# Fourier tables in seven steps between the first loads, the last gate and value by token halves, and a fixed TensorE order through the convolution's second half

## The chip, the core and the metric

The program runs on one core of one Trainium2 chip. The metric is the device time in microseconds (us) of one execution; the time before is 1710.61 us, the median of three runs (1710.35 to 1713.78). The core's engines run side by side, each through its own list of instructions in order, and wait for each other by semaphores: TensorE (PE) multiplies matrices, VectorE (DVE) and ScalarE (ACT) work elementwise, GpSimd (POOL) fills tables, and SyncE's queue (SP) issues the loads.

## The reference

Two layers over 256 latent and 256 context tokens of width 1024. Layer 0 mixes tokens by a Conformer convolution, layer 1 by a bidirectional mLSTM; both are followed by a squared-ReLU MLP. The change touches layer 0's convolution and what comes just before it. In short:

```python
sh1, sc1, g1, sh2, sc2, g2 = adaln(c, ada_w[0], ada_b[0])   # the context has its own six, from c_ctx
u = h * (1 + sc1) + sh1
a = u @ w_pw1 + b_pw1
a = a[..., :1024] * sigmoid(a[..., 1024:])     # value times gate
a = dwconv(a, w_dw)       # 31 taps per channel; latent tokens in rows of 64, context as one row of 256
a = silu(layer_norm(a + b_dw, ln_g, ln_b))
y = a @ w_pw2 + b_pw2
h = layer_norm(ALPHA * h + g1 * y, ln1_g[0], ln1_b[0])
...
```

## The kernel before, in words

All 512 tokens (context in columns 0 to 255, latent in 256 to 511) stand as the free axis; channels stand in 8 tiles of 128 partitions. Matrix products run in three terms: weights and data are each split into a rounded part (`wh`, made by ACT in line 154) and a rest (`wl`, made by DVE in line 155), and `mm3` (lines 177, 180, 181) adds `wh` by `u`, `wh` by `u`'s rest, and `wl` by `u`. Weights come in loads of 1 MB into `raw`, which has three buffers; `wh` and `wl` have four each.

The scheduler decides the order on each engine from the order of the program and its own estimates; the order holds from then on. A matmul may be nailed to its place in the program's order (`keep_in_program_order`, while `pin[0]` is true).

**The start.** Eight rounds `f`: `start0(f)` loads a block of the adaLN weights, a tile of `x` and a block of the first gate and value weights (`wr`), and multiplies the adaLN block with the conditioning columns (`ada_mm`, line 319); DVE copies the sums out of PSUM (line 605); `start1` folds them (line 327), adds the biases (lines 610, 611) and makes `u[f]` and its rest (lines 522, 523, 525); `start2` adds the round's 12 matmuls to four accumulators. PE's order in a round is: fold, the adaLN products of the next round, the 12 matmuls of the round before. Ahead of all this in the program stand the Fourier tables: five tables of 128 x 128 in one tile, `tab`, computed by DVE as sines by a polynomial in lines 556 to 573. GpSimd then makes three masked copies of the first table (`ge32`, `lt32`, `ge96`).

**The first half of the convolution.** A `gemm_steps` loop makes the other 12 gate and value tiles in six groups of two: the even ones are gates (sigmoid on ACT, line 639), the odd ones values (line 643 on DVE multiplies value by gate; PE transposes the tile, line 646; ACT copies it to `A`, line 647, tokens on partitions). Between them DVE runs the row products of adaLN (`ada0.step`, line 379). Once four channel tiles are there, `spectral(0, tt)` convolves 512 channels of each block of 128 tokens: a forward transform (lines 661 and 666, an fp32 matmul by `F0` or a masked copy), a product with the transformed taps on DVE (lines 676, 677), an inverse transform (line 687; two matmuls on different columns of the array, which may run at the same time where they follow each other), and bias and statistics (lines 694, 695).

**The second half.** After the last group `spectral(1, tt)` does the same for the other 512 channels; `token_norm` computes mean and scale of two token blocks on DVE (lines 499 to 505 and around them) and applies them on ACT (line 709); `silu` transposes each channel tile back (line 729), applies gain, bias and SiLU, and splits the result; the gemm with `pw2` takes it, context half first. `ada_sh.mm()` multiplies two further adaLN blocks in that stretch.

## Time and profile before

| | |
|---|---|
| median of three runs | 1710.61 us |
| the profiled execution's own time | 1710.9 us |
| its span, first to last instruction | 1709.2 us |
| DVE busy in the span | 1095.9 us (64%) |
| ACT busy in the span | 743.3 us (43%) |
| GpSimd busy in the span | 33.5 us (2%) |
| DMA, mean over the span | 176 GB/s |

The chain of work that ended last is PE for 90% of the span, DVE for 4%, ACT for 3% and DMA for 2%. PE's row on the page counts modelled ends of pipelined matmuls, so it cannot tell a dense stretch from one at half the clock; windows and the timeline can. In the timeline a row gives start, duration, engine, line, operation, tiles written and read, form and count, and in brackets how long the engine idled before it and who ended that. An fp32 matmul shows as two records. In a windows row each engine's busy time and count stand in the order PE, PE's weight loads, DVE, ACT, POOL, followed by PE's granted clock, the DMA share and GB/s.

### The profile page before, as it was taken

To read this page: it belongs to the slowest core of one execution; us is meant where nothing else is said; L and a number is where in the kernel's file an instruction comes from. 1 tells how busy PE (TensorE), PEld (TensorE's weight loads), DVE (VectorE), ACT (ScalarE), POOL (GpSimd) and SP (SyncE) were. 2 spreads that over 40 slices of the span, in tenths; PEclk is the share of its full clock that TensorE was granted. 3 is DMA by queue.
4 is the path that set the end of the run, shared out by engine and by line. 5 is a ranking of instruction groups with operands and counts; after the bars stand their busy time and mean duration, and the time that the engine had idled before them with its cause. 6 is when DMAs were issued, how large, how long until landed. Compare 5 with 4: busy or idle time off the path is not lost.

```text
span 1709.2 us, 22611 instructions
## 1 busy us (share of the span) xinstructions
PE 1666.7 (98%) x8805; PEld 1365.7 (80%) x8805; DVE 1095.9 (64%) x1971; ACT 743.3 (43%) x1196; POOL 33.5 (2%) x84
## 2 busy tenths in 40 slices
PE   5999999999999999999999999999999999999998
PEld 3755788888888998876678889888867778888886
DVE  6895797975666686773132553453387786678765
ACT  2412565132324364643232543342276674555652
POOL 1000000000000000000000000000011110000000
PEclk9999999999999999999999999999999999999999
DMA  8634214555554236557663542253355545646651
GB/s 316 248 123 179 92 51 175 219 211 207 197 197 172 75 119 196 179 197 267 234 222 123 194 154 93 101 195 124 123 185 190 205 173 204 243 182 222 234 186 48
DMA packets 60666, 301.57 MB, mean 176 GB/s; under 512 B 6066, under 2 KB 20946, under 8 KB 27152
## 3 DMA queue, kind: packets, MB, share of 16 engines
q1 hardware_dynamic: 42832, 285.44, 46.0%
q10 hardware_dynamic: 17728, 14.70, 2.6%
q8 instruction: 69, 1.13, 0.3%
q14 instruction: 37, 0.30, 0.1%
HBM read 284.37 MB, written 15.75 MB: 176 GB/s over the span
## 4 chain that ended last, share of the span: by engine, by line
PE 90%; DVE 4%; ACT 3%; DMA 2%; issue 1%; POOL 0%; SPq 0%; DVEq 0%; ACTq 0%; POOLq 0%
PE mm L177 17%; PE mm L180 17%; PE mm L181 16%; PE mm L192 4%; PE mm L187 3%; PE mm L185 3%; PE mm L1544 3%; PE mm L186 3%; PE mm L196 2%; PE cv L185 2%; PE cv L187 2%; PE cv L186 2%; PE mm L1545 2%; PE cv L687 1%; DVE wl L155 1%; PE fl L797 1%
## 5 line engine op out<-in xcount | busy, mean ns | idle before, releaser
L155 DVE TENSOR_TENSOR wl<-raw,wh 128x1024 fp32r<-128x1024 f32 x346 | 422.0, 1224 | 303.9 <-ACT wh L154 301.3
L154 ACT CAST wh<-raw 128x1024 fp32r<-128x1024 f32 x346 | 360.9, 1052 | 508.8 <-PE mm L180 307.0
L180 PE MATMUL mm<-u,wh 128*128 128x512 f32 (+1 forms) x832 | 298.1, 360 | 0.0
L177 PE MATMUL mm<-u,wh 128*128 128x512 f32 (+1 forms) x704 | 248.1, 357 | 5.8 <-DVE E L967 3.3
L181 PE MATMUL mm<-u,wl 128*128 128x512 f32 (+1 forms) x704 | 248.1, 355 | 0.0
L180 PEld LDWEIGHTS mm<-u,wh 128*128 128x128 f32 x832 | 157.8, 190 | 24.0 <-issue 1.6
L177 PEld LDWEIGHTS mm<-u,wh 128*128 128x128 f32 x704 | 132.4, 190 | 31.8 <-issue 4.4
L181 PEld LDWEIGHTS mm<-u,wl 128*128 128x128 f32 x704 | 133.5, 190 | 19.8 <-issue 2.2
L177 PE MATMUL mm<-xm,wh 128*128 128x512 f32 x256 | 102.8, 402 | 0.0
L185 PE MATMUL mm<-wh,xl 128*128 128x512 f32 x256 | 101.2, 397 | 0.7 <-ACT wh L154 0.5
L186 PE MATMUL mm<-wh,xl 128*128 128x512 f32 x256 | 100.4, 392 | 0.6 <-DVE xl L155 0.6
L181 PE MATMUL mm<-xm,wl 128*128 128x512 f32 x256 | 100.3, 392 | 0.0
L187 PE MATMUL mm<-wl,xl 128*128 128x512 f32 x256 | 99.6, 394 | 0.3 <-DVE wl L155 0.2
L379 DVE CUSTOM_DVE_ANT_0 raw<-raw,cb,vecs 128x1024 f32<-128x1024 f32 x64 | 81.7, 1282 | 25.8 <-DMA raw<-adar_w 25.3
L177 PE MATMUL mm<-hid,wh 128*128 128x512 f32 (+1 forms) x256 | 93.2, 364 | 0.0
L180 PE MATMUL mm<-hid,wh 128*128 128x512 f32 (+1 forms) x256 | 92.8, 363 | 0.0
L181 PE MATMUL mm<-hid,wl 128*128 128x512 f32 (+1 forms) x256 | 92.8, 363 | 0.0
L1544 PE MATMUL mm<-x,wh 128*128 128x512 f32 x224 | 79.0, 397 | 0.0
L180 PE MATMUL mm<-qq,wh 128*128 128x272 f32 x256 | 73.9, 289 | 0.0
L177 PE MATMUL mm<-qq,wh 128*128 128x272 f32 x256 | 73.5, 289 | 0.0
L181 PE MATMUL mm<-qq,wl 128*128 128x272 f32 x256 | 73.5, 288 | 0.0
L192 PE MATMUL mm<-u,wh 128*128 128x512 f32 x192 | 68.4, 398 | 0.0
(490 smaller groups left out, 3277.8 us busy)
## 6 DMA issues: line engine op xcount, KB each, us to landing
raw<-w SPq DMA_DIRECT2D x64, 1024.0 KB, 4.8
raw<-adar_w SPq DMA_DIRECT2D x32, 1024.0 KB, 4.8
raw<-wo SPq DMA_DIRECT2D x32, 1024.0 KB, 4.8
raw<-ada_w SPq DMA_DIRECT2D x16, 1024.0 KB, 4.9
raw<-wv SPq DMA_DIRECT2D x16, 1024.0 KB, 5.3
raw<-wqT SPq DMA_DIRECT2D x16, 1024.0 KB, 5.8
raw<-wq SPq DMA_DIRECT2D x16, 1024.0 KB, 4.8
raw<-wk SPq DMA_DIRECT2D x16, 1024.0 KB, 4.8
```

The lines of the kernel that those rows point to most:

```text
L154: c = nc.scalar.copy(hi, src)
L155: nc.vector.tensor_tensor(lo, src, hi.bitcast(F32), op=ALU.subtract)
L177: a = nc.tensor.matmul(ps, wh, xh, start=start, stop=False)
L180: nc.tensor.matmul(ps, wh, xl, start=False, stop=False)
L181: nc.tensor.matmul(ps, wl, xh, start=False, stop=stop)
L185: nc.tensor.matmul(ps, xh, wh, start=start, stop=False)
L186: nc.tensor.matmul(ps, xl, wh, start=False, stop=False)
L187: nc.tensor.matmul(ps, xh, wl, start=False, stop=stop)
L192: nc.tensor.matmul(ps, wh, x, start=start, stop=stop)
L196: nc.tensor.matmul(ps[:, :C], wl, x[:, :C], start=False, stop=False)
L379: nc.vector.tensor_tensor_reduce(dump, w, cb[:, s, :], 1.0, vecs[:, o:o + 1], ALU.mult, ALU.add, accum_out=ada[self.l][:, m, s:s + 1])
L1544: a = lambda stop: nc.tensor.matmul(ps, wh, u2[kt], start=kt == 0, stop=stop)
```

## The change

Four edits in the function that builds the program.

1. The tables become a generator, `tables()`. Its body stands where the tables stood, but its steps run inside the start's rounds, one behind each `start2`; seven pieces in all, first the table arguments, then three pieces for `WC` and `WS`, then three for `F0`, `G1` and `G2` (before, `F0`, `G1` and `G2` came first). The masked copies move behind the start.
2. `spectral(0, tt)` is called one gemm tile later, behind tile 4 of the loop instead of inside the value tile 3, and the row products are dealt out as (1, 2, 1, 2, 2, 2, 2, 2, 1, 1) over ten tiles.
3. The sixth group of gate and value leaves the loop. Its two tiles are made in halves of 256 tokens, with matmuls of 256 columns, and sigmoid, product, transposes and copy work on a half each.
4. From there to the end of the adaLN products PE's order is nailed to the program's, which is written out by hand: the forward transforms of token blocks 0 and 1 between the halves of the last value tile, the inverse ones after it, and one `ada_sh.mm()` between the forward and inverse transforms of each of blocks 2 and 3. `silu(0)` follows, with its affine now on ACT for both halves, and `token_norm(2)` stands right behind it.

```diff
-    for t_ in (tab[:, 0:3 * L], tab[:, 3 * L:5 * L]):
...
+    def tables():
...
+        yield
+        for t_ in (tab[:, 3 * L:5 * L], tab[:, 0:3 * L]):
...
+            nc.vector.scalar_tensor_tensor(tz, t_, -1.0, t_, op0=ALU.mult, op1=ALU.max)
+            yield
...
+            nc.vector.scalar_tensor_tensor(tz, tz, SIN[4], sq_, op0=ALU.add, op1=ALU.mult)
+            yield
+            for k in (3, 2, 1):
+                nc.vector.scalar_tensor_tensor(tz, tz, SIN[k], sq_, op0=ALU.add, op1=ALU.mult)
+            nc.vector.scalar_tensor_tensor(t_, tz, SIN[0], t_, op0=ALU.add, op1=ALU.mult)
+            yield
+
+    tabs = tables()
...
         if f >= 2:
             start2(f - 2)
+            next(tabs, None)
     pin[0] = False
+    for _ in tabs:
+        pass
...
-        if f == 3:
-            for tt in range(4):
-                spectral(0, tt)
...
-            if s:
-                nc.scalar.activation(y, xn, AF.Identity, scale=V("cln_g", f), bias=V("cln_b", f))
-            else:
-                nc.vector.tensor_scalar(y, xn, V("cln_g", f), V("cln_b", f), op0=ALU.mult, op1=ALU.add)
+            nc.scalar.activation(y, xn, AF.Identity, scale=V("cln_g", f), bias=V("cln_b", f))
...
         pw1_epi(m + KO0, ps)
-        ada0.step(2 if m % 3 == 2 else 1)
+        if m == 4:
+            for tt in range(4):
+                for _ in spectral(0, tt):
+                    pass
+        ada0.step((1, 2, 1, 2, 2, 2, 2, 2, 1, 1)[m])
...
-    steps = gemm_steps(pw1, range(6), u, T, pw1_next)
+    steps = gemm_steps(pw1, range(5), u, T, pw1_next)
...
-    normed = None
-    for t0 in (0, 2):
-        for tt in (t0, t0 + 1):
-            spectral(1, tt, normed)
-        normed = token_norm(t0)
-        if t0 == 0:
-            for g in range(2):
-                pre_pw2(g)
-            for _ in silu(0):
-                pass
-    for i in range(2):
+    def pw1_part(m, s, kts=range(DT)):
+        sl = HALVES[s][1]
+        for kt in kts:
+            mm3(ps2[m][:, sl], *kcol(wl2[m], kt), *[t_[:, sl] for t_ in u[kt]], kt == 0, kt == DT - 1)
...
+    pin[0] = True
+    for m in range(2):
+        pw1_part(m, 0)
+        if m == 0:
+            part_epi(0, 0)
+    pw1_part(0, 1, range(4))
+    part_epi(1, 0)
+    pw1_part(0, 1, range(4, DT))
+    part_epi(0, 1)
+    pre_pw2(0)
+    sp = [spectral(1, tt, banks=("mm", "fl")) for tt in range(2)]
+    next(sp[0])
+    pw1_part(1, 1, range(4))
+    next(sp[1])
+    pw1_part(1, 1, range(4, DT))
+    for _ in sp[0]:
+        pass
+    part_epi(1, 1)
+    for _ in sp[1]:
+        pass
+    normed = token_norm(0)
+    pre_pw2(1)
+    for tt in (2, 3):
+        sp1 = spectral(1, tt, normed)
+        next(sp1)
         ada_sh.mm()
+        for _ in sp1:
+            pass
     ada_sh.end()
+    pin[0] = False
+    for _ in silu(0):
+        pass
+    token_norm(2)
```

DVE's list at the start of the program, before: `tab` and its helpers `F_143`, `F_157` are the tables, `fl_194` holds the sums of the first adaLN products, and `F_203` is their copy, which the first fold on PE reads.

```order
L568 TENSOR_SCALAR tab<-F_157 128x256
L572 SCALAR_TENSOR_TENSOR F_143<-F_143,F_144 128x384
L569 TENSOR_TENSOR F_158<-tab 128x256
L573 SCALAR_TENSOR_TENSOR tab<-F_143,tab 128x384
L570 TENSOR_SCALAR F_157<-F_158 128x256
L605 COPY F_203<-fl_194 128x256
L572 SCALAR_TENSOR_TENSOR F_157<-F_157,F_158 128x256
L610 TENSOR_SCALAR sh1p<-ln_205,vecs 128x2
```

The same place in the list now: the copy of the sums (line 600 of the changed kernel) stands behind the split of the first weight block and one multiplication for the tables.

```order
L551 TENSOR_SCALAR pc<-pc 128x1
L155 TENSOR_TENSOR wl_174<-wr_147,wh_173 128x512
L145 TENSOR_TENSOR foldg<-foldg,ident 128x16
L552 TENSOR_TENSOR pc<-pc 128x1
L557 TENSOR_SCALAR tab<-F_121,pc 128x128
L553 TENSOR_SCALAR pc<-pc 128x1
L600 COPY F_158<-fl_149 128x256
L558 TENSOR_SCALAR tab<-F_121,pc 128x128
L605 TENSOR_SCALAR sh1p<-ln_160,vecs 128x2
```

Of the 25 operations of the tables that stood ahead of the first copy one still does; the others stand behind it, spread over the rounds.

PE's list where the second half's normalized tokens come, before: `u_557` and `u_559` are the normalized blocks, which line 729 transposes, `cv_1358` and `cv_1377` the inverse transforms of blocks 2 and 3, `mm_1445` the first `pw2` tile.

```order
L327 MATMUL fl_1432<-fold,F_1430 128x4 x4
L729 MATMUL ln_1270<-ident,u_557 128x128
L729 MATMUL ln_1289<-ident,u_557 128x128
L666 MATMUL mm_1365<-A,tab 128x512
L729 MATMUL ln_1270<-ident,u_559 128x128
L729 MATMUL ln_1289<-ident,u_559 128x128
L687 MATMUL cv_1358<-F_1354,tab 64x512
L687 MATMUL cv_1358<-F_1350,tab 64x512
L687 MATMUL cv_1358<-F_1355,tab 64x512
L729 MATMUL ln_1270<-ident,u_557 128x128
L729 MATMUL ln_1270<-ident,u_559 128x128
L687 MATMUL cv_1358<-F_1351,tab 64x512
```

The same place now (the inverse transforms are line 701, the transposes line 743, the forward transforms line 680, `cv_1284` is token block 1 and `cv_1347` block 2):

```order
L701 MATMUL cv_1284<-F_1257,tab 64x512
L701 MATMUL cv_1284<-F_1253,tab 64x512
L680 MATMUL mm_1323<-A,tab 128x512
L680 MATMUL mm_1322<-A,tab 128x512
L319 MATMUL fl_1334<-raw_1335,cs 32x512 x4
L319 MATMUL fl_1334<-raw_1337,cs 32x512 x4
L743 MATMUL ln_1393<-ident,u_557 128x128
L743 MATMUL ln_1412<-ident,u_557 128x128
L743 MATMUL ln_1393<-ident,u_559 128x128
L743 MATMUL ln_1412<-ident,u_559 128x128
L701 MATMUL cv_1347<-F_1330,tab 64x512
L701 MATMUL cv_1347<-F_1326,tab 64x512
```

The four inverse matmuls of a block now follow each other, and between the last inverse transform of block 1 and the first transpose of the normalized block stand two forward matmuls and eight adaLN products, nothing else.

PE's list where five gate and value tiles of the first half's loop are done, now: `mm_767` is tile 4 of the loop, `ln_753` the transposes of tile 3's value, `mm_802` the first forward transform (line 675).

```order
L177 MATMUL mm_767<-u_199,wh_771 128x512
L180 MATMUL mm_767<-u_200,wh_771 128x512
L181 MATMUL mm_767<-u_199,wl_772 128x512
L658 MATMUL ln_753<-ident,E_719 128x128 x4
L177 MATMUL mm_767<-u_251,wh_771 128x512
...
L181 MATMUL mm_767<-u_505,wl_772 128x512
L675 MATMUL mm_802<-A,ge_545 128x512
```

Before, the same transposes stood right behind tile 3's last matmul and the forward transform right behind them; now 18 matmuls of tile 4 stand between the two, and 6 ahead of the transposes.

## The prediction

> **What bounds the kernel now.** I read the page first, then PE's waits, then windows on the stretches where PE waits, then the timeline there.

> ```profile
> span 1709.2 us, 22611 instructions
> PE 1666.7 (98%) x8805; PEld 1365.7 (80%) x8805; DVE 1095.9 (64%) x1971; ACT 743.3 (43%) x1196; POOL 33.5 (2%) x84
> ```

> PE is the bound nearly everywhere, so time can only be won where PE waits or is slow. Its own waits by releaser over the whole span show that the stretch which the change touches holds the longest ones (us in total, times, longest):

> ```profile
> PE ln L327 <- DVE F L605: 11.7, 2, 10.3
> PE ln L729 <- ACT u L709: 1.6, 1, 1.6
> PE ln L646 <- DVE E L643: 1.3, 1, 1.3
> PE mm L661 <- ACT A L647: 1.2, 1, 1.2
> PE fl L327 <- DVE F L353: 0.8, 1, 0.8
> ```

> The first is the start: a fold waits 10.3 us for DVE's copy of 512 bytes a partition. The next two belong to the second half and to the point before `spectral(0)`. They cost more than their length, as windows laid on the steps of the granted clock show:

> ```profile
> 23.54:26.95 3.41, 3.41 (x20) 1.88 (x21) 2.62 (x7) 1.09 (x2) 0.00 (x0) 1.00 0.71 238
> 81.56:84.97 3.41, 1.00 (x7) 0.45 (x5) 3.41 (x7) 2.48 (x3) 0.00 (x0) 1.00 0.74 303
> 84.97:88.39 3.42, 3.42 (x4) 1.47 (x5) 2.12 (x7) 0.00 (x0) 0.00 (x0) 0.50 0.89 309
> 166.90:170.31 3.41, 2.00 (x18) 1.00 (x11) 1.90 (x13) 0.00 (x0) 0.00 (x0) 1.00 0.89 317
> 170.31:173.72 3.41, 2.42 (x4) 0.79 (x4) 3.07 (x6) 2.94 (x4) 0.00 (x0) 0.50 1.01 425
> 173.72:177.13 3.41, 3.41 (x8) 1.05 (x8) 1.13 (x2) 0.56 (x1) 0.00 (x0) 0.50 0.45 185
> ```

> After a window in which PE was busy for 1.00 of 3.41 us, and after one with 2.00 of 3.41, the next was granted half the clock: one window long (84.97 to 88.39) and two (170.31 to 177.13). At half clock 3.41 us do the work of 1.71, so these dips cost 1.7 and 3.4 us.

> **Term 1, the start.** The timeline, before:

> ```profile
> 6.17 1.94 PE L319 MATMUL fl<-raw,cs 128*32 128x256 f32 x16 [1.05 <-DMA raw<-ada_w]
> 8.13 0.69 DVE L155 TENSOR_TENSOR wl<-wr,wh 128x512 fp32r<-128x512 f32 x1 [0.71 <-ACT wh L154]
> 11.33 0.62 ACT L154 CAST wh<-wr 128x512 fp32r<-128x512 f32 x1 [3.23 <-DMA wr<-pw1a]
> 15.20 0.62 ACT L154 CAST wh<-wr 128x512 fp32r<-128x512 f32 x1 [3.25 <-DMA wr<-pw1a]
> 17.89 0.42 DVE L605 COPY F<-fl 128x256 f32<-128x256 f32 x1
> 18.36 1.01 PE L327 MATMUL ln<-fold,F 128*128 128x2 f32 x4 [10.25 <-DVE F L605]
> 25.54 0.79 PE L177 MATMUL mm<-u,wh 128*128 128x512 f32 x1
> 26.98 0.39 PE L177 MATMUL mm<-u,wh 128*128 128x512 f32 x1
> ```

> The adaLN products are done at 8.1, and the copy stands behind the tables until 17.89. In the new list it stands behind the split that starts at 8.13 and four small operations: at about 9.3, and the fold at 9.8. That would be 8.6 us earlier, but then loads pace the start: casts 3.87 us apart (11.33, 15.20) mean a round's three loads every 3.87 us, so the third block's products start no earlier than 6.17 + 2 x 3.87 = 13.9, and in PE's list they follow the second fold, which needs the second products (10.0 to 12.7), their copy and 1 us of fold: 14.4. They end at 16.3, and the first of the 12 matmuls stands there instead of at 25.54: 9.2 us. The first three took 1.44 us (25.54 to 26.98), where three take 0.69 later. The records show no lower grant there, but the pace changes at the end of the first window that PE filled (23.54 to 26.95). With PE busy from 9.8 on, this should be gone: 0.75 more. From there the round sets the pace:

> ```profile
> 33.34 0.50 PE L327 MATMUL ln<-fold,F 128*128 128x2 f32 x4
> 50.49 0.50 PE L327 MATMUL ln<-fold,F 128*128 128x2 f32 x4
> 42.45 0.22 DVE L610 TENSOR_SCALAR sh1p<-ln,vecs 128x2 f32<-128x2 f32 x1 [1.48 <-PE ln L327]
> 8.74 0.35 DVE L564 TENSOR_SCALAR F<-tab 128x384 f32<-128x384 f32 x1
> 10.12 0.56 DVE L567 SCALAR_TENSOR_TENSOR F<-tab 128x384 f32<-128x384 f32 x1
> 14.13 0.55 DVE L572 SCALAR_TENSOR_TENSOR F<-F,F 128x384 f32<-128x384 f32 x1
> ```

> Four rounds in 17.15 us are 4.29 each, and DVE idles 1.48 of each. The wide table steps need more than that: two of 0.35 and two of 0.56 us (1.8), about the same again, and four of 0.55 (2.2), 5.8 against 4.4. So DVE ends the start 1.4 us late, and the last round's matmuls wait for it (`u`'s rest, line 525): minus 1.4. Nothing else covers this; with full cover it is 0, and had the steps all to be paid on the path it is the whole 5.8. **Term 1: 9.2 + 0.75 - 1.4 = 8.5.** The queue is not in the way: `raw` is freed by the products, two rounds ahead of need.

> **Term 2, up to the end of the first half.** The value tile 3 waits behind DVE's row products:

> ```profile
> L379 DVE CUSTOM_DVE_ANT_0 raw<-raw,cb,vecs 128x1024 f32<-128x1024 f32 x8 | 10.3, 1283 | 0.2
> L155 DVE TENSOR_TENSOR wl<-raw,wh 128x1024 fp32r<-128x1024 f32 x5 | 6.1, 1223 | 0.8 <-ACT wh L154 0.8
> 106.59 0.39 PE L177 MATMUL mm<-u,wh 128*128 128x512 f32 x1
> 107.97 0.39 PE L177 MATMUL mm<-u,wh 128*128 128x512 f32 x1
> ```

> Now 6 matmuls cover the product and 18 the copy (six starts between the last two rows are 1.38 us, so 0.23 each: 1.4 and 4.1 us): the waits of 1.3 and 1.2 go, and with them the dip of 1.7. What is late next is DVE: 20 row products of 1.2 us, four splits of 1.15 and 2.1 of small work from its start of the stretch stand ahead of the first product with the taps, some 31 us, where PE needs 33 for its matmuls; the copies that free accumulators then cost about 0.5. So 1.3 + 1.2 + 1.7 - 0.5 = **3.7**.

> The scheduler's new order also adds waits. The value products of tiles 5 and 9 now stand right ahead of their transposes (tile 9's with no matmul between), and in DVE's list a `wl` split or the `x` updates stand before them. Each costs PE at least about 0.75 and at most 0.75 + 1.22; I take 1.1 for each, so **minus 2.2**, of 0 to 4.

> **Term 3, the second half.**

> ```profile
> 151.05 1.07 PE L319 MATMUL fl<-raw,cs 128*32 128x512 f32 x8
> 158.10 1.94 PE L687 MATMUL cv<-F,tab 128*64 128x512 f32 x8
> 165.83 0.17 DVE L499 TENSOR_SCALAR mw<-mv 128x2 f32<-128x2 f32 x1
> 170.43 2.94 ACT L709 ACTIVATE u<-u,mw 128x512 f32<-128x512 f32 x4 [17.11 <-DVE mw L705]
> 180.86 1.07 PE L687 MATMUL cv<-F,tab 128*64 128x512 f32 x2
> 194.57 0.28 PE L177 MATMUL cv<-u,wh 128*128 128x256 f32 x1
> 194.93 0.28 PE L177 MATMUL cv<-u,wh 128*128 128x256 f32 x1
> 197.81 0.30 PE L177 MATMUL mm<-u,hid 128*128 128x256 f32 x1
> ```

> From the first adaLN product (151.05) to the fifth `pw2` tile (197.81) PE takes 46.8 us. Its work there is 35.2: inverse transforms in pairs at 1.94 per block, 96 matmuls of 256 columns at 0.12 (three start in 0.36), the rest by their rows. The other 11.6 are the two waits of the list above (2.4), the dip (3.4), inverse and forward matmuls that ran alone (1.07 for the two records of one, where four beside each other take 1.94) instead of beside their pair (six and two: 4.2), and 1.6 in pieces. The nailed order brings the pairs together: 4.2 gone. The adaLN fold's wait gets covered, but the wait for the normalized block stays. The chain is fixed: bias and statistics of block 1 (four operations of 0.6 to 0.7 with the last `wl` split among them, 3.6), 13 small operations at 0.2 (2.6), ACT's first 0.73. Before, from line 499 to ACT were 4.6, with other work inside. That is 6 to 7 us, against 3.2 of forward transforms and adaLN products in the list: PE waits about 2.7, and 0.5 more for ACT's second block. By the windows above, that brings a dip again: 1.7 or 3.4, I take 2.5. The halved tiles cost 96 matmuls at 0.12 for 48 at 0.227: 0.6. ACT's share grows by an affine for each tile, but with 1.2 us a tile it stays under PE's 1.4; 0.3. Sum: 11.6 - (2.7 + 0.5 + 2.5 + 0.6 + 0.3) = **5.0**.

> [...]

> **Term 4, `pw2`'s second half.** PE's waits from 197 to 262 are five, this the longest (sum 2.9):

> ```profile
> PE mm L181 <- DVE hid L155: 0.8, 1, 0.8
> ```

> `token_norm(2)` now runs while PE is in the context half, so part of them should go: between 0 and 2.9, **1.5**.

> Sum: 8.5 + 3.7 - 2.2 + 5.0 + 1.5 = 16.5 us. From the profiled execution's 1710.9 that gives 1694.4, and the median of the runs lies 0.3 under it: 1694.1, say 1694. What follows the convolution is unchanged and shifts as a whole, since its loads are issued as buffers come free.

> **Rivals.**
> [...]
> - *The tables stay on the path*: DVE takes them in turn, and each step stands ahead of a copy or of `u`'s rest. Then the 5.8 of wide steps is paid: 4.4 more than forecast, 1698.5. For it speaks that only 1.48 a round is free; against it that folds come a round of 2.7 us of matmuls after the copy.
> - *DVE bounds the first half*: a late row-product load holds DVE's list back before the taps, and the gain of term 2 becomes a loss. The margin is only 2 us; one load late by 5 us gives 1699.
> - *What is won is lost later*, another queue being the limit behind the convolution (DMA or DVE): I see no such wait in the list above, so perhaps half of it, 1702.
> - *Slower than before*: the nailed order keeps PE below the share of busy time that restores the clock, and it stays at half through the second half, from the wait for the normalized block on. Each window costs 1.71, so it decides from the tenth on (16.5 / 1.71); from there to the end of `pw2`'s context half lie some 35 us; with twelve windows, 1715. Against it: 173.72 to 177.13, one busy window, restored it.

> **How the numbers follow.** Forecast 0.52, no dip 0.18, tables on the path 0.12, DVE bound 0.08, lost later 0.06, slower 0.04. The range runs from 1687.5 (no dip, no new waits, all of term 4) to 1702. A measurement of this kernel tells 0.2% (3.4 us) from no change; all cases but the last are faster by more, but half of "lost later" could miss it: 0.93, 0.03, 0.04.

> **What would show it.** In the changed kernel's profile: the first fold near 10, the first `mm` matmul near 16.5, the last round's end near 48 instead of 56; no wait at the transposes before `spectral(0)` and no half clock there, but short waits at two later value tiles; inverse matmuls only in fours; a wait of 2 to 3 us at line 743's first transpose with half a clock behind it. Wrong would be a start whose folds wait for line 600, a first forward transform that waits for DVE, or a gain that is seen at the end of the convolution and not at the end of the span.

## The result, and the profile after

The changed kernel took 1695.84 us, median of four runs (1694.68 to 1697.14), against 1711.14 us before in the same rounds (1710.35 to 1713.78): a ratio of 0.9908, 95% interval 0.9891 to 0.9925. It is 15.3 us faster; 1694 was forecast, within 1687.5 to 1702. The profiled execution took 1694.68 us, 16.2 less than the profiled one before, where 16.5 was forecast.

The page after, its first line and TensorE's:

```profile
span 1693.0 us, 22721 instructions
PE 1661.1 (98%) x8853; PEld 1366.3 (81%) x8853; DVE 1092.0 (65%) x1964; ACT 745.7 (44%) x1206; POOL 33.4 (2%) x84
```

TensorE's waits of 0.5 us and more after, from the start to the end of `pw2` (us in total, times, longest). One of 4.7 us, which is older than the change, is left out:

```profile
PE ln L743 <- ACT u L723: 3.1, 1, 3.1
PE ln L327 <- DVE F L600: 2.1, 2, 1.5
PE fl L319 <- DMA raw<-ada_w: 1.6, 1, 1.6
PE ln L658 <- ACT wh L154: 0.9, 1, 0.9
PE mm L675 <- DVE F L691: 0.8, 1, 0.8
PE mm L180 <- DVE u L525: 0.6, 1, 0.6
PE mm L181 <- DVE wl L155: 0.5, 1, 0.5
```

The fold's 10.3 us became 1.5, and the two waits around the first half's first forward transform are gone. The wait for the normalized block grew from 1.6 to 3.1. New are one at the last value tile of the loop (line 658; the list names ACT, but the transposes follow DVE's product of line 655, and in `spectral_after_tile3` below the same wait stands under it), and three for DVE up to the end of the first half (lines 675, 180 and 181). Windows laid on the steps of the granted clock, around the wait of 3.1:

```profile
150.75:154.17 3.42, 3.42 (x20) 0.87 (x20) 3.42 (x7) 0.00 (x0) 0.00 (x0) 1.00 0.07 12
154.17:157.58 3.41, 1.15 (x12) 0.13 (x4) 2.92 (x16) 0.07 (x1) 0.00 (x0) 1.00 0.96 363
157.58:160.99 3.41, 2.60 (x8) 1.11 (x10) 2.27 (x4) 3.41 (x6) 0.00 (x0) 0.50 0.97 392
160.99:164.41 3.42, 3.42 (x10) 0.74 (x6) 1.12 (x2) 0.35 (x1) 0.00 (x0) 0.50 0.38 161
164.41:167.82 3.41, 3.07 (x24) 0.81 (x22) 2.83 (x5) 0.60 (x2) 0.00 (x0) 1.00 0.25 41
```

One window with 1.15 us of work was followed by two at half the clock. The dip at the first forward transform, one window before, has no counterpart.

To see which stretch won what, the program is cut at matmuls that every kernel here has. TensorE's timeline gives them; first before, then after (start, duration):

```profile
62.88 0.69 PE L771 MATMUL ln<-F,tab 31*128 31x512 f32 x1
...
128.49 0.69 PE L771 MATMUL ln<-F,tab 31*128 31x512 f32 x1
...
241.61 0.28 PE L181 MATMUL mm<-u,hid 128*128 128x256 f32 x1
```

```profile
41.38 0.28 PE L327 MATMUL ln<-fold,F 128*128 128x2 f32 x2
...
55.03 0.69 PE L786 MATMUL ln<-F,tab 31*128 31x512 f32 x1
...
118.38 0.69 PE L786 MATMUL ln<-F,tab 31*128 31x512 f32 x1
...
184.45 0.39 PE L177 MATMUL mm<-u,hid 128*128 128x256 f32 x1
...
225.10 0.28 PE L181 MATMUL mm<-u,hid 128*128 128x256 f32 x1
```

The cuts are the last matmul of the start's last fold (0.25 us behind its row: 50.74 before, 41.63 after), the first and the second set of taps (lines 771 and 786), and the first and the last `pw2` matmul with `hid`. The last stretch goes to the end of the last matmul; in every kernel the span ends 8.3 us later. With the experiments told below, in us, from one profiled execution of each kernel; the median is that of all its runs:

| kernel | last fold at | to 1st taps | to 2nd taps | to 1st `hid` | to last `hid` | to the last matmul's end | median |
|---|---|---|---|---|---|---|---|
| before | 50.74 | 12.14 | 65.61 | 69.32 | 43.80 | 1459.3 | 1711.1 |
| the change | 41.63 | 13.41 | 63.34 | 66.07 | 40.65 | 1459.6 | 1695.8 |
| tables_alone | 42.23 | 13.43 | 64.97 | 69.48 | 43.81 | 1459.6 | 1703.2 |
| tables_first | 50.78 | 12.14 | 61.22 | 66.13 | 40.66 | 1459.1 | 1702.7 |
| spectral_after_tile3 | 41.25 | 13.40 | 63.45 | 66.21 | 40.67 | 1459.9 | 1695.6 |
| free_order | 41.54 | 13.44 | 63.31 | 64.93 | 40.66 | 1460.0 | 1692.9 |
| filler_1 | 42.58 | 13.41 | 63.34 | 65.21 | 40.66 | 1461.3 | 1695.3 |
| filler_3 | 41.30 | 13.40 | 63.33 | 63.55 | 40.68 | 1461.4 | 1693.8 |
| inverse_earlier | 41.55 | 13.41 | 63.31 | 64.20 | 40.69 | 1459.6 | 1692.5 |
| rows_later | 42.11 | 13.41 | 60.87 | 66.24 | 40.67 | 1458.8 | 1692.5 |
| rows_later_tables_held | 42.71 | 13.20 | 61.15 | 64.80 | 40.68 | 1460.5 | 1693.0 |
| inverse_earlier_rows_later | 42.05 | 13.43 | 60.85 | 63.78 | 40.67 | 1459.7 | 1692.2 |
| all_three | 42.06 | 13.19 | 61.15 | 63.58 | 40.68 | 1460.8 | 1691.4 |
| tables_on_gpsimd | 42.12 | 13.28 | 60.85 | 63.77 | 40.65 | 1460.8 | 1689.5 |

From before to the change: 9.1 up to the last fold, 1.3 lost up to the first taps, then 2.3, 3.3 and 3.1 won, 0.3 lost in the rest: 16.2. Two columns also tell what a median is worth here. The rest of the program, which no kernel touches, takes 1458.8 to 1461.4 us, and kernels with the same start reach the last fold between 41.25 and 42.58. So a difference of a microsecond between medians says little, and the stretches are what is read. The column "to last `hid`" shows how steady a stretch is that nothing disturbs: 40.65 to 40.69 in all kernels with the fourth edit.

### The profile page after: what moved, and what is told of

It reads as the page before. It is cut to its first block, busy times and chain, and to the rows that moved or that the text cites. A ratio compares the mean times of both kernels' runs of the same rounds, so it can differ in the third digit from the quotient of the medians.

```text
span 1693.0 us, 22721 instructions
## 1 busy us (share of the span) xinstructions
PE 1661.1 (98%) x8853; PEld 1366.3 (81%) x8853; DVE 1092.0 (65%) x1964; ACT 745.7 (44%) x1206; POOL 33.4 (2%) x84
## 3 DMA queue, kind: packets, MB, share of 16 engines
q8 instruction: 70, 1.15, 0.3%
## 4 chain that ended last, share of the span: by engine, by line
PE 91%; DVE 5%; ACT 2%; issue 1%; DMA 1%; POOL 0%; SPq 0%; DVEq 0%; ACTq 0%; POOLq 0%
PE mm L177 17%; PE mm L180 17%; PE mm L181 17%; PE mm L192 4%; PE mm L187 3%; PE mm L185 3%; PE mm L1591 3%; PE mm L186 3%; PE mm L196 2%; PE cv L187 2%; PE cv L186 2%; PE cv L185 2%; PE mm L1592 2%; DVE wl L155 1%; PE fl L812 1%; PE ln L177 1%
## 5 line engine op out<-in xcount | busy, mean ns | idle before, releaser
L155 DVE TENSOR_TENSOR wl<-raw,wh 128x1024 fp32r<-128x1024 f32 x346 | 421.8, 1223 | 306.4 <-ACT wh L154 303.3
L154 ACT CAST wh<-raw 128x1024 fp32r<-128x1024 f32 x346 | 360.4, 1050 | 483.4 <-PE mm L180 286.3
L180 PE MATMUL mm<-u,wh 128*128 128x512 f32 (+1 forms) x848 | 301.8, 357 | 1.0 <-DVE u L525 0.6
L177 PE MATMUL mm<-u,wh 128*128 128x512 f32 (+1 forms) x720 | 253.6, 355 | 3.8 <-DVE E L1014 3.2
L181 PE MATMUL mm<-u,wl 128*128 128x512 f32 (+1 forms) x720 | 250.5, 350 | 0.5 <-DVE wl L155 0.5
L180 PEld LDWEIGHTS mm<-u,wh 128*128 128x128 f32 x848 | 161.1, 190 | 24.5 <-issue 1.8
L177 PEld LDWEIGHTS mm<-u,wh 128*128 128x128 f32 x720 | 136.1, 190 | 28.5 <-issue 5.1
L181 PEld LDWEIGHTS mm<-u,wl 128*128 128x128 f32 x720 | 136.8, 190 | 19.9 <-issue 1.4
L177 PE MATMUL mm<-xm,wh 128*128 128x512 f32 x256 | 102.8, 402 | 0.0
L181 PE MATMUL mm<-xm,wl 128*128 128x512 f32 x256 | 100.3, 392 | 0.0
L379 DVE CUSTOM_DVE_ANT_0 raw<-raw,cb,vecs 128x1024 f32<-128x1024 f32 x64 | 81.6, 1281 | 24.1 <-DMA raw<-adar_w 23.6
L177 PE MATMUL mm<-hid,wh 128*128 128x512 f32 (+1 forms) x256 | 93.2, 364 | 0.0
L181 PE MATMUL mm<-hid,wl 128*128 128x512 f32 (+1 forms) x256 | 92.8, 363 | 0.0
L181 PE MATMUL mm<-qq,wl 128*128 128x272 f32 x256 | 73.5, 288 | 0.0
L177 PE MATMUL mm<-qq,wh 128*128 128x272 f32 x256 | 73.5, 288 | 0.0
```

Source lines behind the costliest of these rows:

```text
L154: c = nc.scalar.copy(hi, src)
L155: nc.vector.tensor_tensor(lo, src, hi.bitcast(F32), op=ALU.subtract)
L177: a = nc.tensor.matmul(ps, wh, xh, start=start, stop=False)
L180: nc.tensor.matmul(ps, wh, xl, start=False, stop=False)
L181: nc.tensor.matmul(ps, wl, xh, start=False, stop=stop)
L379: nc.vector.tensor_tensor_reduce(dump, w, cb[:, s, :], 1.0, vecs[:, o:o + 1], ALU.mult, ALU.add, accum_out=ada[self.l][:, m, s:s + 1])
```

## The experiments

**One part alone, or one part undone.** Four kernels. `tables_alone` is the kernel before with the first edit, the generator as shown under the change and its calls:

```diff
...
         if f >= 2:
             start2(f - 2)
+            next(tabs, None)
...
```

> The kernel before with the tables' edit alone. Theory (the start's gain is a pure shift that is kept to the end): the trace of the changed kernel shows 7.85 us less from its start to the first taps, so 1711.1 - 7.85 = 1703.3 us. Rival (the table steps or the loads take it back behind the start, in the convolution's first half): 1707 or more, with the first taps at 55.0 us but the first forward transform late.

Measured: 1703.24 us (1701.19 to 1703.88), ratio 0.9956 (0.9943 to 0.9968). The shift is kept to the end. But between the taps only 0.6 us were won (64.97 against 65.61), less than the 1.3 lost ahead of them, and the first half still has a half clock:

```profile
73.80:77.21 3.41, 1.51 (x8) 0.79 (x6) 3.41 (x8) 0.55 (x1) 0.00 (x0) 1.00 0.92 322
77.21:80.62 3.41, 3.23 (x4) 1.50 (x5) 2.40 (x4) 2.03 (x3) 0.00 (x0) 0.50 0.69 281
```

`tables_first` is the change with the tables in front of the start again:

```diff
-    def tables():
...
+    for t_ in (tab[:, 0:3 * L], tab[:, 3 * L:5 * L]):
...
-            next(tabs, None)
```

> The changed kernel with the tables in front of the start again, the other edits kept. Theory (independent terms): 1695.8 + 7.85 = 1703.7 us. Rival (the other edits pay only with the early start, or the reverse): under 1701 or over 1706 us.

Measured: 1702.72 us (1699.29 to 1704.4), ratio 0.9953 (0.9939 to 0.9966). The terms look independent in the sum, and the stretches show that they aren't. With the tables in front TensorE needs 12.14 + 61.22 us from the last fold to the second taps and waits for nothing that the list of waits shows between the taps; with the tables inside the start it needs 13.41 + 63.34. **Beside the other edits, the first one costs 3.4 us behind the start**, out of the 9.1 that it wins; alone it costs 0.65 there. DVE is behind by that work: at the first taps it has begun 3 of the row products of line 379 in the change, and 5 with the tables in front.

`spectral_after_tile3` undoes the move of the first half's spectral blocks:

```diff
-        if m == 4:
+        if m == 3:
             for tt in range(4):
                 for _ in spectral(0, tt):
```

> The changed kernel with the four spectral blocks of the first half behind tile 3 again, the row products dealt as in the change. Theory: the waits at the transposes and at the first forward transform (1.3 + 1.2) and the half clock (1.7) come back, the waits at the value tiles of 5 and 9 (0.5 + 0.4 and 1.1) go: +4.2 - 2.0, 1698.0 us. Rival A: the waits at tiles 5 and 9 come from the dealing and stay: +4.2, 1700.0 us. Rival B: the windows of the clock fall elsewhere with the earlier start and no dip comes: +2.5 or less, 1696 to 1698 us with clock 1.0 throughout the stretch.

Measured: 1695.64 us (1694.86 to 1696.54), ratio 0.9914 (0.99 to 0.9927), the same as the change. Rival B is right in half: the waits of 1.3 and 0.8 came back, but no half clock; they fell into two windows:

```profile
71.99:75.40 3.41, 2.12 (x12) 1.49 (x10) 3.10 (x5) 0.00 (x0) 0.00 (x0) 1.00 0.92 384
75.40:78.82 3.42, 2.65 (x9) 1.25 (x7) 3.38 (x7) 1.61 (x3) 0.00 (x0) 1.00 0.60 218
```

Nearly the same two waits (1.32 and 0.77 us there, 1.29 and 0.77 here) lay in one window in `tables_alone`, with 1.51 us of work, and cost one at half the clock. The transposes and the transform that waited start at 75.97 and 77.39 us there, with windows from 73.80 and 77.21; here they start at 74.97 and 76.39, with windows from 71.99 and 75.40: in these two traces the grid lies differently against the program. And the stretch between the taps is 63.45, as with the move (63.34): with the tables inside the start, the move is worth nothing in these two executions. DVE sets this stretch then, wherever TensorE's list has the transforms (`rows_later`, below). With the tables in front the second edit is worth 4.4 (65.61 to 61.22), a half clock of 1.7 among them. The wait at the last value tile of the loop stayed, so it doesn't come from the move.

`free_order` leaves TensorE's order to the scheduler:

```diff
-    pin[0] = True
+    pin[0] = False
     for m in range(2):
         pw1_part(m, 0)
```

> The changed kernel with TensorE's order left to the scheduler from the last value tile on; the halves and the order of the program stay. Theory of the prediction (the nailed order brings the pairs of inverse matmuls together, 4.2 us): about 1700 us, with inverse matmuls that run alone. Rival (the pairs come from the new order of the program, and the nailed order only holds back the forward transforms of block 3): the wait for the normalized block is 1.1 us shorter, 2.0 instead of 3.1, and the half clock lasts one window instead of two or none: 1692 to 1695 us.

Measured: 1692.9 us (1692.72 to 1693.88), ratio 0.9899 (0.9885 to 0.9912). The rival holds. The inverse matmuls stand in fours here too, but for the last block's, which stand in two pairs; block 3's forward transforms and part of the second adaLN products moved ahead of the normalized block, and the wait for it is gone from the list, where 2.0 were expected. The half clock that is left has another wait behind it, 1.1 us for the first `pw2` matmuls' data:

```profile
154.53:157.94 3.41, 2.86 (x8) 0.72 (x6) 3.10 (x13) 1.55 (x3) 0.00 (x0) 1.00 1.01 394
...
164.77:168.19 3.42, 2.23 (x17) 1.91 (x18) 2.85 (x9) 3.13 (x7) 0.00 (x0) 1.00 1.00 424
168.19:171.60 3.41, 3.41 (x19) 3.41 (x18) 2.95 (x15) 2.08 (x5) 0.00 (x0) 0.50 0.02 10
```

**What brings the half clock.** Matmuls whose result nobody uses, in the place where TensorE waits for the normalized block; `filler_1` has one, `filler_3` three:

```diff
         ada_sh.mm()
+        if tt == 2:
+            idle = psum("ln")
+            for _ in range(3):
+                pe(nc.tensor.matmul(idle, ident, tab[:, 0:512], start=True, stop=True))
```

> The changed kernel with one idle-time matmul of 512 columns (0.86 us, its result is not used) behind the adaLN products, where TensorE waits 3.06 us for the normalized block. Theory (half a clock follows a window of 3.41 us in which TensorE worked 2.2 us or less): 2.2 us of waiting are left, enough for half the clock wherever they fall in one window: 1694 to 1696 us, wait 2.2, half clock for one or two windows. [...]

> The same with three such matmuls (2.6 us): 0.5 us of waiting are left. Theory: no window under 2.2 us of work, so no half clock there, and the chain that TensorE waits for is unchanged: 1695.8 - 3.4 = 1692.4 us, wait 0.5. Rival (the half clock comes from what runs there, not from the wait): half clock as before, 1695.8 us.

Measured: 1695.34 us (1693.63 to 1697.44) and 1693.8 us (1693.71 to 1693.84), ratios 0.9908 (0.9892 to 0.9924) and 0.9899 (0.9882 to 0.9915). With one, a half clock is left (160.18 to 163.59); with three, none, though the normalized block comes no sooner (ACT begins it 39.1 us behind the second taps in the change and in both of these). First `filler_1`, then `filler_3`:

```profile
156.76:160.18 3.42, 1.15 (x5) 0.35 (x4) 3.14 (x13) 1.72 (x3) 0.00 (x0) 1.00 1.01 398
160.18:163.59 3.41, 3.41 (x10) 0.82 (x9) 1.05 (x3) 2.11 (x4) 0.00 (x0) 0.50 0.80 334
```

```profile
154.07:157.48 3.41, 3.41 (x18) 1.06 (x6) 2.92 (x16) 0.32 (x1) 0.00 (x0) 1.00 0.93 339
157.48:160.89 3.41, 2.86 (x13) 0.89 (x12) 2.03 (x4) 3.41 (x6) 0.00 (x0) 1.00 1.00 413
```

The stretch to the first `hid` falls from 66.07 to 63.55: the wait's consequence cost 2.5 us. So idle time brought the half clock, and 2.3 us of it, left by one filler, were enough. The median fell 2.0, to 1693.8 instead of the expected 1692.4. In `filler_3`'s profiled execution 1.8 us more than in the change's lie in the part that no edit touches, which covers the difference; its other three runs have no trace.

**Real work in place of the filler.** `inverse_earlier`:

```diff
     next(sp[1])
+    for tt in range(2):
+        for _ in sp[tt]:
+            pass
     pw1_part(1, 1, range(4, DT))
-    for _ in sp[0]:
-        pass
+    ada_sh.mm()
     part_epi(1, 1)
-    for _ in sp[1]:
-        pass
     normed = token_norm(0)
...
-        ada_sh.mm()
+        if tt == 3:
+            ada_sh.mm()
```

> The changed kernel with the inverse transforms of blocks 0 and 1 ahead of the last 12 matmuls of the last value tile, and the first adaLN products ahead of that tile's transposes, so that 1.4 us of matmuls and 1.8 us of adaLN products that the normalized block doesn't need stand behind the statistics instead of ahead. Theory (the wait is 5.9 us of chain less the work behind the statistics): wait 0.5 or less, no half clock: 1695.8 - 3.1 - 3.4 + 0.5 = 1689.8 us. Rival A (DVE is late with the taps' products of block 1, so the inverse transforms wait instead, 1 to 2 us, and the half clock stays): 1694 us. Rival B (the adaLN loads are late for the earlier products): a wait for a load there, 1693 us or more.

Measured: 1692.46 us (1691.71 to 1695.3), ratio 0.9894 (0.9878 to 0.9909). The wait fell from 3.1 to 1.4, not to 0.5, and a window at half the clock stayed (157.60 to 161.01, behind one with 1.67 us of work). Rival A came in part: two inverse transforms wait 0.9 us together. The chain on DVE in the changed kernel's timeline shows where the time goes (the last row is ACT's):

```profile
150.92 0.68 DVE L708 TENSOR_TENSOR u<-cv,bdw 128x512 f32<-128x512 f32 x1
151.52 1.22 DVE L155 TENSOR_TENSOR wl<-raw,wh 128x1024 fp32r<-128x1024 f32 x1
152.65 0.69 DVE L709 BATCH_NORM_STATS2 bst<-u 128x6 f32<-128x512 f32 x1
153.26 0.67 DVE L708 TENSOR_TENSOR u<-cv,bdw 128x512 f32<-128x512 f32 x1
...
157.30 0.17 DVE L719 TENSOR_SCALAR mw<-mw 128x2 f32<-128x2 f32 x1
...
157.51 2.93 ACT L723 ACTIVATE u<-u,mw 128x512 f32<-128x512 f32 x4 [6.78 <-DVE mw L719]
```

A weight split of 1.22 us, whose data TensorE reads some 20 us later, stands in the middle of it; in `inverse_earlier` it stood there too, among the small operations.

`rows_later` moves four of twenty row products behind the first half's spectral blocks:

```diff
-        ada0.step((1, 2, 1, 2, 2, 2, 2, 2, 1, 1)[m])
-        if m == 5:
+        ada0.step((0, 1, 1, 1, 1, 2, 2, 2, 3, 3)[m])
+        if m == 6:
```

> The changed kernel with four of the twenty row products (1.28 us each) moved from ahead of the first half's spectral blocks to behind them. Theory (the table steps have made DVE the bound of the first half: from its first taps to its second 63.35 us, against 61.22 with the tables in front): the waits at line 675 (0.8) and at tile 5 (0.5 + 0.4) go, 63.35 becomes 61.3 to 61.8, 1693.9 us. Rival (those waits come from the order of the lists, not from DVE's amount of work): 63.3 as before, 1695.8 us, or later waits of the same size at tiles 7 to 9.

Measured: 1692.46 us (1691.19 to 1694.73), ratio 0.9892 (0.9877 to 0.9907). As the theory had it, with a little more: 63.34 became 60.87. Of the three waits for DVE in the first half one is left:

```profile
PE mm L180 <- DVE u L525: 0.5, 1, 0.5
```

**What is lost between the last fold and the first taps.** In the change the last steps of the tables stand on DVE ahead of `u`'s rest (line 525), for which TensorE waits (0.9 of the 1.3 us go there, by the starts of its matmuls, and 0.3 at a weight split behind it):

```profile
44.13 0.41 DVE L523 TENSOR_SCALAR S<-x,sc1p,sh1p 128x256 f32<-128x256 f32 x1
44.45 0.55 DVE L577 SCALAR_TENSOR_TENSOR F<-F,F 128x384 f32<-128x384 f32 x1
44.92 0.69 DVE L525 TENSOR_TENSOR u<-S,u 128x512 fp32r<-128x512 f32 x1
```

`rows_later_tables_held` keeps them behind that rest (`st["rest"]` is the subtraction of line 525):

```diff
...
-            next(tabs, None)
+            if f < 7:
+                next(tabs, None)
     pin[0] = False
-    for _ in tabs:
-        pass
+    with tc.issue_after(st["rest"].ins):
+        for _ in tabs:
+            pass
```

> The kernel rows_later, with the last steps of the tables (one piece and a half of the seven, 4.2 us of DVE) held back until DVE has made the rest of the last block of u. Theory (from the last fold to the first taps TensorE takes 13.41 us with the tables in the start and 12.14 without, because these steps stand ahead of that rest): 13.41 becomes 12.2, the second taps stay at 60.9 after the first since four row products are gone from there, 1692.5 - 1.2 = 1691.3 us. Rival A (the 4.2 us of steps make the first half late again): 12.2, but 61.5 to 62.5 up to the second taps, 1692.0 to 1692.5 us. Rival B (the 1.27 us have another cause): 13.4 as before.

Measured: 1692.97 us (1692.44 to 1693.03), ratio 0.989 (0.9876 to 0.9905). The wait for `u`'s rest went, and two matmuls more (0.5 us) run ahead of the first taps. But up to the second taps it is 13.20 + 61.15 = 74.35 against 13.41 + 60.87 = 74.28 in `rows_later`: nothing. The steps delay what stands behind them instead: TensorE now waits 0.3 us for a rounded weight and 0.7 us for DVE's products with the taps. That is rival A, in the sum.

**Together.** `inverse_earlier_rows_later` has both and takes the split out of the chain:

```diff
-    pre_pw2(0)
+    raw0 = raw_load(pw2[0, 0])
+    pre2[0] = split_w(raw0[:, 0:1024])
...
     normed = token_norm(0)
-    pre_pw2(1)
+    pre2[1] = split_w(raw0[:, 1024:2048])
...
+        if tt == 3:
+            ada_sh.mm()
+            pre_pw2(1)
```

> inverse_earlier and rows_later together, with the second load of pw2 behind the last adaLN load, so that its split (1.22 us) leaves the chain between the statistics of block 1 and the normalized block. Theory (the two gains are in different stretches and add; the wait of 1.4 was 1.2 of split): rows_later 1692.5 less 3.1 to 5.2: 1687.3 to 1689.4 us, wait under 0.5, no half clock at the normalized block. Rival A (the chain's next member, DVE's products of block 1 that wait for buffers, 2.0 us, holds it): wait 1 and half a clock for a window, 1690.5 us. Rival B (pw2's second load is now late for the first pw2 tiles): a wait for it at line 154 or 177 of 1 to 4 us, 1691 us or more.

`all_three` adds the held tables.

> Both together: the held tables, the later row products, the earlier inverse transforms and the later pw2 load. Theory (all terms are in stretches of their own): 1.2 us less than inverse_earlier_rows_later. Rival (DVE has no room for the held steps): the same time as it.

Measured: 1692.19 us (1690.47 to 1693.34) and 1691.42 us (1690.38 to 1692.82), ratios 0.9886 (0.9871 to 0.99) and 0.9883 (0.9866 to 0.9899). The half clock at the normalized block is gone and its wait is two of 0.4 or less; the stretches are the sums of the parts (60.85; 63.78 against 64.20 and 66.24). But 2.5 us were won over `rows_later` in the stretch, not 3.1 to 5.2, since short waits took the place of the long one: 1.3 us for the taps' products in three pieces, 1.1 for the normalized block's second transposes, 0.5 for a copy. In the medians the gain is not to be seen. The held tables won 0.1 up to the first `hid`, which is the rival's answer.

`tables_on_gpsimd` puts the last two pieces of the wide table group on GpSimd:

```diff
+            eng = nc.vector if t_.shape[-1] == 2 * L else nc.gpsimd
...
-            nc.vector.tensor_tensor(sq_, t_, t_, op=ALU.mult)
+            eng.tensor_tensor(sq_, t_, t_, op=ALU.mult)
```

> The kernel inverse_earlier_rows_later, with the last two pieces of the wide table group (8 steps, 4.2 us on DVE) on GpSimd, there as 14 steps. Theory (the 1.27 us between the last fold and the first taps are DVE's amount of work: held back, the same steps delayed the product of the first value tile instead): 13.43 becomes 12.1 to 12.2, 60.85 to the second taps stays or falls to 60.6, 1692.2 - 1.3 = 1690.9 us. [...] Rival B (GpSimd takes so long that the masked copies of the first table are late for the first forward transform, due 37 us after the last fold): a wait at that transform, 1692 us or more.

Measured: 1689.52 us (1688.36 to 1691.57), ratio 0.9871 (0.9854 to 0.9887), the lowest of all. The stretches don't explain the lower median: 13.28, 60.85 and 63.77, where `inverse_earlier_rows_later` has 13.43, 60.85 and 63.78. They are those of the slowest of the four runs (1691.57); why the others were faster stays open. Of the 1.3 us in the theory 0.15 were won up to the first taps, though eight steps, 4.0 us, left DVE's list. The wait for `u`'s rest went, and one for a weight split took its place. That split took 1.82 us, where it took 1.22 without work on GpSimd (last section):

```profile
47.86 1.82 DVE L155 TENSOR_TENSOR wl<-raw,wh 128x1024 fp32r<-128x1024 f32 x1
49.73 0.50 PE L181 MATMUL mm<-u,wl 128*128 128x512 f32 x1 [0.60 <-DVE wl L155]
```

## Why the prediction was right, and where it wasn't

The time was right, and so were the mechanisms at the start and at the normalized block. The terms were off by 0.3 to 1.7 us, in both directions, and two reasons were wrong. That the sum came so near is in part luck: terms 1 to 3 brought 1.6 us less than forecast, and term 4 brought 1.65 more. The lower end of the range is 1688.0 by the terms named for it, not 1687.5.

**Term 1** (8.5 forecast, 7.85 measured up to the first taps: 62.88 against 55.03). The first fold came at 10.19 (about 9.8 forecast), the first `mm` matmul at 16.42 (16.3). TensorE waits for no load once the first adaLN products have begun, so the chain of products, copy and fold paces this stretch (the third products start at 14.55, 14.4 forecast), not the loads. DVE's lateness up to the first taps was sized right: 1.3 us against 1.4. What failed is the 0.75 for the first matmuls:

```profile
16.42 0.80 PE L177 MATMUL mm<-u,wh 128*128 128x512 f32 x1
17.01 0.63 PE L180 MATMUL mm<-u,wh 128*128 128x512 f32 x1
17.44 0.49 PE L181 MATMUL mm<-u,wl 128*128 128x512 f32 x1
17.76 0.40 PE L177 MATMUL mm<-u,wh 128*128 128x512 f32 x1
```

Three took 1.34 us instead of 1.44. "With PE busy from 9.8 on" was wrong: TensorE still waits 1.5 us and less at the folds until 13.6, and the trace's first clock record, at the full clock, begins at 17.63.

**Term 2** (3.7, less 2.2 for new waits at two value tiles). Between the taps 2.3 were won, and the wait at the last tile of the loop, which lies behind the second taps, took about 1.1: 1.2 against the 1.5 forecast. The sum is near, its parts aren't. The 1.3 + 1.2 + 1.7 are there, 4.4 us, but only with the tables in front. In the change 2.1 of them go to DVE, which is late by the table steps. The prediction named DVE as what is late next, gave it 0.5, and made more of it a rival of 0.08, with a late load as the cause. The step that failed is the count of DVE's work ahead of the taps: it took 31 against 33 us as a margin and left out that DVE comes out of the start with steps of the tables unpaid: its first row product starts 9.4 us behind the last fold, and 6.6 with the tables in front. All told, the tables inside the start cost 3.4 us behind it, where 1.4 was put down. The wait at tile 5 was put down to the scheduler's order; it was 0.5, not 1.1, and goes with four row products less, so it is DVE's work too. The wait at the loop's last tile is none of the second edit's: it stays with the spectral blocks moved back, and it goes in `free_order`, where the scheduler put eight matmuls of the halves between that tile and its transposes. And the 1.7 of the clock was not the move's alone to win: nearly the same waits cost it in `tables_alone` and not in `spectral_after_tile3`, by where the windows lie (1.51 us of work in one, against 2.12 and 2.65 in two).

**Term 3** (5.0; measured 3.25 to the first `hid`, or about 4.3 without the wait at the loop's last tile, which was counted in term 2). The wait was forecast at 2.7 and is 3.1, its dip at 2.5 and cost 2.5. (The chain of 6 to 7 us less 3.2 gives 2.8 to 3.8, so 2.7 lay under its own bounds.) The reason given for the gain was wrong in one point: "the nailed order brings the pairs together". Without it the fours stay, so the program's new order and the halves bring them (no run parts the two); the nailed order only holds back block 3's forward transforms and costs 1.1 us (66.07 against 64.93).

No run shows what no dip at this wait would rest on; it got 0.18 and stands in the lower end of the range. In the change a dip came after a window with 1.15 us of work (154.17 to 157.58); with work in the gap there was none (`filler_3`: 3.41 and 2.86 us of work in the two windows there, both at the full clock).

**Term 4** (1.5, of 0 to 2.9; measured 3.15). All of the waits in `pw2`'s second half went and a little more. The traces fit the mechanism: `token_norm(2)` begins on DVE at 172.51, 11.9 us ahead of the first `hid` matmul, where it began 0.2 us ahead of it before (197.57). But no run parts this from the affine that moved to ACT, so the cause isn't shown. The size was taken too low: nothing in the profile spoke for half.

Of the rivals, no dip and a slower second half did not come, nothing was lost later (0.3 us in the rest), and two came in part: DVE bounds the first half (2.1 us), and the tables stay on the path, 3.4 us in all (those 2.1 and the 1.3 up to the first taps), mainly not ahead of the folds but behind the start. Of the signs of being wrong one came, in small: the first two folds still wait for line 600, 2.1 us together.

## What to carry to other kernels

Work that leaves a waiting engine's path still has to be done by someone: count the engine's whole work up to the next place where it is waited for, not only the idle time in the stretch that it moves to. A wait of a few microseconds in TensorE costs itself and perhaps one or two windows at half the clock: in the windows listed below, 1.67 us of work or less in 3.41 brought it each time, 2.00 to 2.35 in two of four. If nothing useful can stand there, even useless matmuls can win (2.5 us of their stretch here). Two edits whose effects add up in the total can still have given and taken in between, so compare stretches cut at the same instructions, above all where medians differ by less than the untouched rest varies.

## What the runs showed of the hardware

Nine windows at the full clock with 0.51 to 1.67 us of work were each followed by half the clock: 0.52, 1.00 and 1.43 before (from 617.45, 81.56 and 1699.48), 0.51, 1.15 and 1.35 after (from 601.31, 154.17 and 1683.34), 1.15 in `filler_1`, 1.51 in `tables_alone` and 1.67 in `inverse_earlier`. Between 2.00 and 2.35 both came: 2.00 before and 2.23 in `free_order` brought it, 2.12 in `spectral_after_tile3` and 2.35 in `inverse_earlier_rows_later` didn't. From the first clock record on, no window of 2.58 or more brought it in the traces before and after. At half the clock, 2.42 before and 2.60 after were followed by half again; 3.06, 3.41 and 3.42 before, 3.08 and 3.42 after, by the full clock. Work is the profile's busy time, whose matmul ends are modelled. Where between these figures a bound lies, and whether work alone sets it, was not shown.

While GpSimd worked on tables of 128 x 384 (38.76 to 57.68 us in `tables_on_gpsimd`), several of DVE's operations took longer, the two below 2 and 1.6 times as long. DVE's groups between 38 and 52 us, first in `inverse_earlier_rows_later`, then in `tables_on_gpsimd` (count, then busy us and mean ns):

```profile
L523 DVE TENSOR_SCALAR S<-x,sc1p,sh1p 128x256 f32<-128x256 f32 x4 | 1.5, 406 | 0.0
...
L379 DVE CUSTOM_DVE_ANT_0 dump<-raw,cb,vecs 128x1024 bf16<-128x1024 f32 x1 | 1.3, 1277 | 0.0
```

```profile
L523 DVE TENSOR_SCALAR S<-x,sc1p,sh1p 128x256 f32<-128x256 f32 x4 | 3.1, 804 | 0.1
...
L379 DVE CUSTOM_DVE_ANT_0 dump<-raw,cb,vecs 128x1024 bf16<-128x1024 f32 x1 | 2.0, 2033 | 0.0
```

GpSimd needed 0.5 to 2.1 us for each of its steps, as spans on GpSimd are read. What made DVE's operations longer was not shown: no run here isolates the cause.
